# A hybrid recurrent decoder step: a larger filling rate per chunk step, and the late work taken at every step where the filling has run out

## The chip, the cores and the metric

The kernel runs on one core of one Trainium2 chip. The metric is the device time of one execution in microseconds (us). The engines are named as the profile names them: PE is TensorE, DVE is VectorE, ACT is ScalarE, POOL is GpSimd, SP issues DMAs.

## What is computed

Two layers work on 512 prompt tokens with 16 learned tokens ahead of them, and on 8 sample tokens that carry states. Each layer is a half feed-forward, a mixer, and a half feed-forward:

```python
for l in range(DEPTH):                       # DEPTH = 2
    x = x + half_ffn(x, ...)                 # 0.5 * (silu(h @ Wg) * (h @ Wu)) @ Wd
    h = rmsnorm(x, prm['norm_mix'][l])
    m = even_mixer(h, ...) if l % 2 == 0 else odd_mixer(h, ...)
    x = x + m
    x = x + half_ffn(x, ...)

def even_mixer(h, ...):
    proj = h @ even_w_in
    # four gated heads:   S_t = diag(f_t) S_{t-1} + k_t v_t^T,  o_t = S_t^T q_t   (128 x 128)
    oa = rmsnorm(gla_seq(q, k, v, logf, ...) * sigmoid(ga), hgrn_norm)
    # eight RWKV-7 heads: S_t = S_{t-1} diag(w_t) + (S_{t-1}(-kk_t)) (kk_t*a_t)^T + v_t k_t^T,
    #                     y_t = S_t r_t                                            (64 x 64)
    ob = (group_norm(y) + bonus) * g
    return concat([oa, ob]) @ even_w_out
```

All of the change lies in the even mixer of layer 0.

## The kernel before

The 536 tokens lie along the free axis; a matrix product in full precision is three matmuls per 128 x 128 block (high by high, low by high, high by low), over two token parts, 0 to 272 and 272 to 536. On tiles called `d` these triples are the dense products; on tiles `w` lies the RWKV recurrence; on tiles `m` the rest.

**The RWKV recurrence** (`waves`) goes through 9 chunks of tokens (one of 16, eight of 64) for two groups of heads, 18 chunk runs. A chunk run opens with `stage_g` (18 matmuls), then inverts a triangular matrix in ten alternating steps (`lev_t` on PE with ACT copies, `lev_x` on PE with a DVE copy), and ends with five output steps (`st_p`, `st_t`, `st_sa`, `st_s`, `st_y`) that carry the state. Three inverses run side by side, and a table fixes the order: 280 steps, numbered 0 to 279 here. The last chunk run opens in step 240, so from step 241 on ever fewer runs are in flight.

**What is put between the steps.** PE's order is the order in which the code of the loop is written out; the other engines are ordered by a scheduler. After each step the loop earns a credit of `FILL` columns, at most `FILL_MAX`, and spends it on the gated heads (`hgrn_thread`): for heads 0 to 3 a chain of advances (`hcore`, 2500 credit each, 1000 for head 3, that is PE scores, DVE masks and products, POOL scalings), and beside them the dense projections of the next head in pieces of 816 or 792 columns (three matmuls). Heads 0 to 2 have a head's projections beside their advances; head 3 has 12 advances and no projection left. When this thread has ended, what is left of the credit goes to the output projection over the first token part (`mix_out`, 8 weight blocks of 24 matmuls, 192 in all), as soon as two things are done: the norm over the gated heads (`hgrn_norm`, "first" in the code) and the RWKV output work of tokens 0 to 272 ("half").

**Those two are in `post`**, a second thread, which is advanced in every third step and charges `POST` (2000) or a quarter of it. It takes the token spans 0 to 272, 272 to 400 and 400 to 536 as the recurrence passes them; for each span `rpost` does two pairs of head groups in four advances each, and each pair holds two reciprocals on DVE. `hgrn_norm` comes in seven advances: squares of the four heads, a matmul with ones, square root, a reciprocal over all tokens, and four scalings.

After the last step what is left of `post` runs, with the rest of `mix_out` put between its advances, and then the output projection over the second token part (192 matmuls in 8 blocks, with weights loaded anew), and the second feed-forward.

```python
def gla_core(...):                                   # one level of an advance, L651 to L662
    scores(li + 1)                                   # PE, then DVE masks
    nc.vector.tensor_mul(qv[:, :, 1], ...)           # L659
    nc.gpsimd.tensor_mul(kv[:, :, 0], ...)           # L660
    nc.vector.tensor_mul(nxt, ...)                   # L662
```

Of the kernel before, what the change touches and what calls it, by code (L numbers as in the profile page):

```python
# [51 lines left out]
NVEC = _r  # L52


FILL, FILL_MAX = 1100, 5000
CORE, CORE_LAST = 2500, 1000
BESIDE = 2000
AHEAD = 12864
# [3 lines left out]
SAMPLE_EVERY, POST_EVERY = 3, 3  # L62
# [46 lines left out]
def trunk(ctx, tc, A, O):  # L109
# [4 lines left out]
    def til(pool, shape, tag, dt=F32, bufs=None):  # L114
        cnt[0] += 1
        kw = {} if bufs is None else {"bufs": bufs}
        return pool.tile(shape, dt, tag=tag, name=f"{tag}_{cnt[0]}", **kw)
# [8 lines left out]
    def psum(**sizes):  # L126
        if sizes == {tag: n for tag, (_, n) in rings.items()}:
            return
        banks.close()
        rings.clear()  # L130
        for tag, n in sizes.items():
            pool = banks.enter_context(tc.tile_pool(name=f"ps{tag}", bufs=n, space=bass.MemoryType.PSUM))
            rings[tag] = (pool, n)
# [457 lines left out]
    def mix_out(w, norm, l, xd, part, mid=None, units=None):  # L591
        for m in range(NK):
            u = unit(w, 0, 128 * m, NK, 2) if units is None else units(m)
            xv = X['x'][:, m]
            if part != PARTS[1]:
                nc.sync.dma_start(xv, xd[m])  # L596
            yield from dense_steps(u, NK, lambda k: hh[:, k], lambda k: hl[:, k],
                                   lambda ps, sl: nc.vector.tensor_add(xv[:, sl], ps, xv[:, sl]), [part], 1)
            if mid is not None and part != PARTS[1] and m == 1:
                mid()  # L600
        norm_split(norm, l, slice(*part))
# [168 lines left out]
    def even_mixer(rstd, xd, left):  # L770
        w_in = A["even_w_in"][0]
        c0 = 2048
        right = ExitStack()
        mx = right.enter_context(tc.tile_pool(name="mx", bufs=1, side="right"))
        g2 = til(mx, [P, 512], "g2")
        lg = til(mx, [P, T], "lg")
        shl = til(mx, [P, 14, 9], "shl")
        R = [dict(sl=til(mx, [P, 5, T], f"sl{p}"), wc=til(mx, [P, 9], f"wc{p}"),
                  ws=til(mx, [P, NB], f"ws{p}"))
             for p in range(4)]  # L780
        for Q in R:
            Q["r"] = Q["sl"][:, 4]
        oa = [til(mx, [P, T], f"oa{h}") for h in range(4)]
        nc.scalar.dma_start(g2, A["rwkv_g2"][0])
        he = ExitStack()
        hp = he.enter_context(tc.tile_pool(name="hp", bufs=1))
        H = {}
        th = hgrn_thread(hp, rstd, w_in, oa, H)
        psum(d=4, m=4)
        with tc.tile_pool(name="etmp", bufs=1, side="right") as tmp:  # L790
            rwkv_in(tmp, rstd, w_in, c0, g2, lg, shl, R, th)
        psum(d=2, m=2, w=4)
        pb = right.enter_context(tc.tile_pool(name="pb", bufs=1, side="right"))
        ts = chain(*(rsample(R[p], p, lambda i: til(npool, [P, T], ("acc", "sq")[i])) for p in range(4)))
        now = [0]


        def hgrn():
            yield from th
            he.close()  # L800
            xp = left.enter_context(tc.tile_pool(name="xp1", bufs=1))
            X['x'] = til(xp, [P, NK, T], "xT")
            now.append("norm")

        def hgrn_end():
            if "norm" in now and "done" not in now:
                now.append("done")
                for _ in hgrn_norm(oa):
                    yield POST // 4
                now.append("first")  # L810

        def post():
            for span in zip(SPANS, SPANS[1:]):
                while 3 not in H or now[0] < 10 and CHUNKS[max(now[0] - 1, 0)][0] < span[1]:
                    yield from hgrn_end()
                    yield 0
                for _ in ts:
                    yield 0
                for p in (0, 2):
                    yield from hgrn_end()  # L820
                    gens = [rpost(i, R[i], g2, lg, *span) for i in (p, p + 1)]
                    while gens:
                        gens = [g for g in gens if next(g, 0) is None]
                        yield POST
                if span[1] >= PARTS[0][1]:
                    now.append("half")

        with tc.manual_schedule(engines={mybir.EngineType.PE}):
            th_, po = hgrn(), post()
            mo = mix_out(A["even_w_out"][0], "norm_ffn2", 0, xd, PARTS[0])  # L830
            credit = FILL_MAX
            for n, w in enumerate(waves(pb, R)):
                now[0] = w
                if n % SAMPLE_EVERY == 0:
                    next(ts, None)
                if n % POST_EVERY == 0:
                    credit -= next(po, 0)
                credit = min(credit + FILL, FILL_MAX)
                while credit > 0:
                    cost = next(th_, None)  # L840
                    if cost is None and "first" in now and "half" in now:
                        cost = next(mo, None)
                    if cost is None:
                        break
                    credit -= cost
            now[0] = 10
            for _ in th_:
                pass
            for _ in po:
                if "first" in now and "half" in now:  # L850
                    credit = MIX
                    while credit > 0:
                        credit -= next(mo, credit)
            for _ in mo:
                pass
        psum(d=4, m=4)
        for _ in mix_out(A["even_w_out"][0], "norm_ffn2", 0, xd, PARTS[1]):
            pass
        right.close()

    def hgrn_norm(oa):
        yield
        acc = squares(oa)
        yield
        yield
        ro = til(npool, [P, T], "rstd", bufs=2)
        sum_to_rstd(acc, 1.0 / 512, ones, ro)
        for k in range(4):
            nc.vector.tensor_mul(oa[k], oa[k], ro)
            gcol = vec("hgrn_norm", k)  # L870
            nc.scalar.activation(hh[:, k], oa[k], AF.Copy, scale=gcol)
            nc.vector.scalar_tensor_tensor(hl[:, k], oa[k], gcol, hh[:, k].bitcast(F32), ALU.mult, ALU.subtract)
            yield
# [467 lines left out]
    def rpost(p, Q, g2, lg, a, b):  # L1341
        n = b - a
        r, k, v, y = (z[:, a:b] for z in (Q["r"], Q["sl"][:, 1], Q["sl"][:, 2], Q["sl"][:, 3]))

        pair_t = til(npool, [P, 2, 272], ("acc", "sq")[p % 2])[:, :, :n]

        def over(lhsT, rhs, fn):
            wide(lhsT, rhs, lambda ps, sl: fn(ps), [(0, n)], "w")

        yc, sq = pair_t[:, 0], pair_t[:, 1]  # L1350
        over(bones, y, lambda ps: nc.vector.scalar_tensor_tensor(yc, ps, -1.0 / 64, y, ALU.mult, ALU.add))
        yield
        nc.scalar.activation(sq, yc, AF.Square)
        over(bones, sq, lambda ps: nc.scalar.activation(y, ps, AF.Sqrt, bias=epst[:, 1:2], scale=1.0 / 64))
        yield
        nc.vector.reciprocal(y, y)
        nc.vector.scalar_tensor_tensor(r, r, vec("rwkv_rk", p), k, ALU.mult, ALU.mult)
        over(bones, r, lambda ps: nc.vector.tensor_mul(sq, ps, v))
        nc.vector.tensor_mul(yc, yc, y)
        yield  # L1360
        nc.vector.tensor_scalar(yc, yc, vec("rwkv_ln_w", p), vec("rwkv_ln_b", p), ALU.mult, ALU.add)
        nc.vector.tensor_add(yc, yc, sq)
        over(g2[:, 128 * p:128 * p + 128], lg[:, a:b], lambda ps: nc.vector.tensor_mul(yc, ps, yc))
        nc.scalar.copy(hh[:, 4 + p, a:b], yc)
        nc.vector.tensor_sub(hl[:, 4 + p, a:b], yc, hh[:, 4 + p, a:b].bitcast(F32))
# [261 lines left out]
    rstd = norm_in("norm_mix", 0)  # L1627
    left.close()
    even_mixer(rstd, xd, left)
    psum(d=4, m=4)  # L1630
    ffn(0, "ffn2", norm_rstd())
# [98 lines left out]
```

## Time and profile before

| | |
|---|---|
| time, median of 3 runs | 2314.42 us (2308.76 to 2318.76) |
| time of the profiled execution | 2311.46 us |
| its span, first to last instruction | 2309.6 us |
| PE busy | 97% |
| DVE busy | 70% |
| ACT busy | 48% |
| the even mixer, step 0 to the end of its output projection | 520 to 921 us |

Busy is the time in which at least one instruction of the engine was under way. Matmuls overlap each other, so a busy PE can still take more work: a dense matmul of 272 columns is shown with some 0.29 us, and in a row of them one starts every 0.125 us. Every matmul of the program has its record in this trace, so the steps can be counted off line by line: step 207 starts at 780.1 us, step 232 at 822.0, step 255 at 841.5, and the last one ends at 870.4.

### The profile page before, as it was taken

How to read it: one execution, taken by the hardware profiler on the slowest of the kernel's cores; microseconds unless marked ns; L12 is line 12 of the kernel's file. 1: busy time of each engine (PE TensorE's matmuls, PEld its weight loads, DVE VectorE, ACT ScalarE, POOL GpSimd, SP SyncE). 2: the span in 40 equal slices, each digit the busy share in tenths (PEclk: the TensorE clock that was granted, in tenths of full speed). 3: DMA queues.
4: the chain of work that ended last, by engine and by line, in shares of the span. 5: the costliest groups of instructions: out<-in, count | busy, mean ns of one | idle time of the engine just before them, and what ended most of it. 6: DMA issues, size and time to landing. Idle time of an engine off the chain costs nothing. (4 is left out here: it accounts for less than half of the span.)

```text
span 2309.6 us, 52355 instructions
## 1 busy us (share of the span) xinstructions
PE 2242.7 (97%) x22000; PEld 2158.7 (93%) x22000; DVE 1623.5 (70%) x2899; ACT 1098.4 (48%) x2128; POOL 141.9 (6%) x192
## 2 busy tenths in 40 slices
PE   8999999998999989999999999999999989999998
PEld 8999999997788778999999999999999889999998
DVE  7858576686556778966757885857666777948576
ACT  6525254375454556444535452525444464525355
POOL 0000000312212100000000000000021210000000
PEclk9999999998999999999999999999999999999999
DMA  6323334223222115242423332333444453333324
GB/s 171 108 76 101 92 92 132 81 65 95 80 63 81 50 50 166 66 119 83 115 78 101 92 104 79 101 93 89 124 122 125 120 152 92 92 92 101 110 85 136
DMA packets 409412, 229.55 MB, mean 99 GB/s; under 512 B 19252, under 2 KB 400501, under 8 KB 409176
## 3 DMA queue, kind: packets, MB, share of 16 engines
q1 hardware_dynamic: 408456, 224.78, 33.8%
q8 instruction: 173, 2.83, 0.5%
q10 hardware_dynamic: 720, 1.42, 0.2%
q14 instruction: 63, 0.52, 0.1%
HBM read 211.19 MB, written 14.97 MB: 98 GB/s over the span
## 5 line engine op out<-in xcount | busy, mean ns | idle before, releaser
L242 PE MATMUL d<-hh,whi 128*128 128x264 f32 (+2 forms) x1136 | 344.6, 304 | 3.5 <-ACT whi L230 1.5
L244 PE MATMUL d<-hh,wlo 128*128 128x264 f32 (+2 forms) x1136 | 326.0, 288 | 2.1 <-DVE wlo L231 2.1
L243 PE MATMUL d<-hl,whi 128*128 128x264 f32 (+2 forms) x1136 | 326.1, 287 | 0.1
L336 PE MATMUL d<-hh,whi 128*128 128x268 f32 (+1 forms) x832 | 237.7, 286 | 1.7 <-ACT hh L189 1.2
L337 PE MATMUL d<-hl,whi 128*128 128x268 f32 (+1 forms) x832 | 238.1, 287 | 0.9 <-DVE hl L190 0.9
L338 PE MATMUL d<-hh,wlo 128*128 128x268 f32 (+1 forms) x832 | 237.9, 286 | 0.0
L242 PEld LDWEIGHTS d<-hh,whi 128*128 128x128 f32 x1136 | 215.6, 190 | 11.5 <-ACT whi L230 2.4
L244 PEld LDWEIGHTS d<-hh,wlo 128*128 128x128 f32 x1136 | 214.8, 189 | 4.5 <-DVE wlo L231 3.8
L243 PEld LDWEIGHTS d<-hl,whi 128*128 128x128 f32 x1136 | 215.9, 190 | 0.9 <-issue 0.3
L336 PE MATMUL d<-hid,whi 128*128 128x264 f32 (+2 forms) x704 | 201.5, 287 | 0.0
L336 PE MATMUL d<-hid,whix 128*128 128x264 f32 (+2 forms) x704 | 201.1, 286 | 0.0
L337 PE MATMUL d<-hid,whix 128*128 128x264 f32 (+2 forms) x704 | 200.8, 285 | 0.0
L337 PE MATMUL d<-hid,whi 128*128 128x264 f32 (+2 forms) x704 | 200.6, 286 | 0.0
L338 PE MATMUL d<-hid,wlox 128*128 128x264 f32 (+2 forms) x704 | 200.6, 285 | 0.0
L338 PE MATMUL d<-hid,wlo 128*128 128x264 f32 (+2 forms) x704 | 200.5, 285 | 0.0
L536 DVE SCALAR_TENSOR_TENSOR xT<-d,xT 128x272 f32<-128x272 f32 (+2 forms) x192 | 82.9, 433 | 166.9 <-PE d L338 166.9
L336 PE MATMUL d<-sumh,whix 128*128 128x268 f32 (+1 forms) x576 | 170.9, 297 | 0.0
L338 PE MATMUL d<-sumh,wlo 128*128 128x268 f32 (+1 forms) x576 | 164.7, 286 | 0.0
L337 PE MATMUL d<-suml,whix 128*128 128x268 f32 (+1 forms) x576 | 164.3, 285 | 0.0
L336 PE MATMUL d<-sumh,whi 128*128 128x268 f32 (+1 forms) x576 | 164.2, 285 | 0.0
L338 PE MATMUL d<-sumh,wlox 128*128 128x268 f32 (+1 forms) x576 | 164.0, 285 | 0.0
L337 PE MATMUL d<-suml,whi 128*128 128x268 f32 (+1 forms) x576 | 164.0, 285 | 0.0
(386 smaller groups left out, 6438.5 us busy)
## 6 DMA issues: line engine op xcount, KB each, us to landing
raw<-in_ffn_gate_dram SPq DMA_DIRECT2D x44, 512.0 KB
raw<-in_ffn_up_dram SPq DMA_DIRECT2D x44, 512.0 KB
rawx<-in_ffn_gate_dram SPq DMA_DIRECT2D x44, 512.0 KB
rawx<-in_ffn_up_dram SPq DMA_DIRECT2D x44, 512.0 KB
raw<-in_ffn_down_dram SPq DMA_DIRECT2D x32, 512.0 KB
rawx<-in_ffn_down_dram SPq DMA_DIRECT2D x32, 512.0 KB
raw<-in_even_w_in_dram SPq DMA_DIRECT2D x30, 512.0 KB
raw<-in_odd_w_in_dram SPq DMA_DIRECT2D x25, 512.0 KB
```

The costliest lines, as they stand in the source:

```text
L242: nc.tensor.matmul(o, hi[:, k], h, start=(k == 0), stop=False)
L243: nc.tensor.matmul(o, hi[:, k], l, start=False, stop=False)
L244: nc.tensor.matmul(o, lo[:, k], h, start=False, stop=(k == nk - 1))
L336: nc.tensor.matmul(o, hi[:, k], rh(k), start=start and k == 0, stop=False, **kw)
L337: nc.tensor.matmul(o, hi[:, k], rl(k), start=False, stop=False, **kw)
L338: nc.tensor.matmul(o, lo[:, k], rh(k), start=False, stop=stop and k == nk - 1, **kw)
L536: nc.vector.scalar_tensor_tensor(xv[:, sl], ps, -0.5, xv[:, sl], ALU.mult, ALU.add)
```

## The change

Two edits. A step earns 1400 instead of 1100, and `post` is also advanced in a step that finds the credit at its limit of 5000, that is in one where nothing was left to fill it.

```diff
-FILL, FILL_MAX = 1100, 5000
+FILL, FILL_MAX = 1400, 5000
...
-                if n % POST_EVERY == 0:
+
+                if n % POST_EVERY == 0 or credit >= FILL_MAX:
                     credit -= next(po, 0)
                 credit = min(credit + FILL, FILL_MAX)
                 while credit > 0:
```

No instruction is added or removed: PE has the same 18,871 matmuls, in another order. Followed through the loop, the places move like this (steps):

| | before | after |
|---|---|---|
| advances of gated heads 0 to 2, with projections | 0 to 206 | 0 to 161 |
| advances of head 3 | 206 to 231 | 162 to 170 |
| norm over the gated heads | 234 to 252 | 178 to 184 |
| output work of span 0 to 272 | 207 to 228 | 185 to 196 |
| first half of the output projection | 57 of 192 matmuls in 255 to 278, 135 after the last step | all 192 in 197 to 231 |
| output work of span 272 to 400 | 255 to 276 | 234 to 247 |
| steps with nothing between them | 232 to 254, but for the norm | 248 to 278 |
| output work of span 400 to 536 | step 279 and after it | the same |

Three places in the order of the built programs. Names are tile names: `acc`, `sq` and `sl` are tiles of a head pair, `rstd` the norm's factor, `oa` a gated head, `xx`, `gm`, `tm`, `t1c`, `pp`, `pd`, `S` belong to the recurrence, `hh`, `hl` and `whi`, `wlo` are the high and low parts of activations and weights.

**DVE, the norm's reciprocals.** Before, in steps 243 to 250:

```order
L168 RECIPROCAL rstd_11028<-rstd_11028 128x272
L168 RECIPROCAL rstd_11028<-rstd_11028 128x264
L1143 COPY_PREDICATED xx_10292<-cu_67,w_11056 128x2x128
L869 TENSOR_TENSOR oa_619_4521<-oa_619_4521,rstd_11028 128x536
L869 TENSOR_TENSOR oa_620_4522<-oa_620_4522,rstd_11028 128x536
L1283 TENSOR_TENSOR S_1647_11074<-w_11069,S_1545_10491 128x256
L872 SCALAR_TENSOR_TENSOR hl_71<-oa_619_4521,vcol_69,hh_70 128x536
L872 SCALAR_TENSOR_TENSOR hl_71<-oa_620_4522,vcol_69,hh_70 128x536
L1143 COPY_PREDICATED xx_10644<-cu_67,w_11078 128x2x128
```

After the change the same two reciprocals are followed by a subtraction (L1352, `acc`), the products with `oa` 619 to 621 and the low parts of 619 and 620, and then, still in steps 185 to 188:

```order
L873 SCALAR_TENSOR_TENSOR hl_71<-oa_621_4523,vcol_69,hh_70 128x536
L870 TENSOR_TENSOR oa_622_4524<-oa_622_4524,rstd_10239 128x536
L1352 SCALAR_TENSOR_TENSOR sq_10299<-w_10300,sl_610_4512 128x272
L1357 RECIPROCAL sl_607_4509<-sl_607_4509 128x272
L873 SCALAR_TENSOR_TENSOR hl_71<-oa_622_4524,vcol_69,hh_70 128x536
L1360 TENSOR_TENSOR acc_10295<-acc_10295,sl_607_4509 128x272
L1357 RECIPROCAL sl_610_4512<-sl_610_4512 128x272
L1231 COPY xx_9309<-w_10339 64x2x64
```

Before, the recurrence's copies (L1143, L1283) stand between the norm's products; now the whole norm and the first pair's two reciprocals (L1357) stand between the last recurrence copy ahead of them and the next, L1231.

**PE, the same place.** Before, the matmul with ones of the norm (L157 on `acc`) in step 243:

```order
L1214 MATMUL w_11014<-cf_66,xx_10644 128x128 x2
L157 MATMUL m_11029<-acc_10926,cf_66 128x272
L157 MATMUL m_11033<-acc_10926,cf_66 128x264
L1268 MATMUL w_11040<-pp_10998,xx_9941 128x128 x2
L1194 MATMUL w_11045<-xx_10956,gm_10957 32x32 x8
L1194 MATMUL w_11056<-t1c_11001,xx_10292 32x32 x8
L1278 MATMUL w_11069<-tm_9944 128x128
```

and now in step 180, with the first advances of span 0 to 272 (L157 on `sl` and `acc`) a few steps on:

```order
L157 MATMUL m_10240<-acc_10209,cf_66 128x272
L157 MATMUL m_10244<-acc_10209,cf_66 128x264
L1195 MATMUL w_10251<-t1c_10178,xx_9662 32x32 x8
L1195 MATMUL w_10264<-t1c_10199,xx_10113 32x32 x8
L1295 MATMUL w_10277<-gm_8978,sa_10196 64x64 x4
L1207 MATMUL w_10287<-xx_9309,gm_9310 64x64 x2
L1215 MATMUL w_10287<-cf_66,xx_9309 128x128 x2
L157 MATMUL w_10296<-sl_607_4509,cf_66 128x272
L157 MATMUL w_10300<-sl_610_4512,cf_66 128x272
L1195 MATMUL w_10303<-xx_9662,gm_9663 32x32 x8
L1215 MATMUL w_10303<-cf_66,xx_9662 128x128 x2
L157 MATMUL w_10318<-acc_10295,cf_66 128x272
```

What stood some 27 steps apart, with the span's advances first, now follows within seven steps, norm first.

**PE, behind the last step.** Before, from the last advance of step 279:

```order
L157 MATMUL w_11522<-sl_607_4509,cf_66 128x136
L157 MATMUL w_11526<-sl_610_4512,cf_66 128x136
L1335 MATMUL w_11529<-cf_66,S_1709_11414 128x128
L1335 MATMUL w_11535<-cf_66,S_1709_11414 128x128
L1335 MATMUL w_11541<-cf_66,S_1729_11507 128x128
L1335 MATMUL w_11547<-cf_66,S_1729_11507 128x128
L157 MATMUL w_11554<-acc_11521,cf_66 128x136
L157 MATMUL w_11558<-sq_11525,cf_66 128x136
L242 MATMUL d_11471<-hh_70,whi_11463 128x272
L243 MATMUL d_11471<-hl_71,whi_11463 128x272
L244 MATMUL d_11471<-hh_70,wlo_11464 128x272
```

and now:

```order
L157 MATMUL w_11729<-sl_607_4509,cf_66 128x136
L157 MATMUL w_11733<-sl_610_4512,cf_66 128x136
L1336 MATMUL w_11736<-cf_66,S_1737_11670 128x128
L1336 MATMUL w_11742<-cf_66,S_1737_11670 128x128
L1336 MATMUL w_11748<-cf_66,S_1749_11717 128x128
L1336 MATMUL w_11754<-cf_66,S_1749_11717 128x128
L157 MATMUL w_11761<-acc_11728,cf_66 128x136
L157 MATMUL w_11765<-sq_11732,cf_66 128x136
L157 MATMUL w_11770<-sl_607_4509,cf_66 128x136
L157 MATMUL w_11776<-sl_610_4512,cf_66 128x136
L157 MATMUL w_11782<-lg_4507,g_604_4506 128x136
L157 MATMUL w_11789<-lg_4507,g_604_4506 128x136
```

The dense triples (`d`) that stood behind the second `L157` pair have gone to steps 197 to 231. Further on the scheduler puts eight matmuls of the second token part between the last advances; 24 others of them it has put into steps 234 to 246.

## Rows read from the trace of the kernel before

**Rows 1.** The page: span, and busy time of each engine over it.
```profile
span 2309.6 us, 52355 instructions
...
PE 2242.7 (97%) x22000; PEld 2158.7 (93%) x22000; DVE 1623.5 (70%) x2899; ACT 1098.4 (48%) x2128; POOL 141.9 (6%) x192
```

**Rows 2.** Busy time by stretch: us, PE, PEld, DVE, ACT, POOL, granted clock, DMA share, GB/s.
```profile
520.00:780.00 260.00, 243.54 (x4261) 206.82 (x4259) 148.03 (x440) 126.92 (x368) 58.34 (x61) 0.95 0.27 75
780.00:822.00 42.00, 35.19 (x650) 28.75 (x650) 36.94 (x99) 22.73 (x61) 8.04 (x11) 0.92 0.16 44
822.00:842.00 20.00, 15.93 (x317) 12.14 (x314) 16.66 (x37) 11.85 (x34) 0.00 (x0) 0.89 0.33 112
842.00:870.00 28.00, 27.02 (x284) 24.09 (x285) 19.82 (x61) 13.09 (x43) 0.00 (x0) 0.96 0.08 24
870.00:894.00 24.00, 22.41 (x174) 21.45 (x175) 20.84 (x55) 13.85 (x39) 0.00 (x0) 1.00 0.51 146
893.00:921.00 28.00, 25.07 (x195) 24.05 (x195) 20.91 (x37) 17.16 (x31) 0.00 (x0) 1.00 0.74 201
```

**Rows 3.** The same for instructions on tiles w: us, PE, PEld, DVE, ACT, clock.
```profile
520.00:780.00 260.00, 147.44 (x2690) 112.23 (x2690) 58.36 (x201) 59.85 (x201) 0.95 0.27 75
...
822.00:842.00 20.00, 15.19 (x313) 11.49 (x310) 5.52 (x20) 6.31 (x23) 0.89 0.33 112
```

**Rows 4.** The same for tiles m, then for tiles d, over the steps 0 to 206.
```profile
520.00:780.00 260.00, 36.85 (x1040) 28.31 (x1040) 17.75 (x72) 9.33 (x24) 0.95 0.27 75
...
520.00:780.00 260.00, 102.86 (x531) 74.84 (x529) 9.96 (x23) 0.00 (x0) 0.95 0.27 75
```

**Rows 5.** Tiles d in the late stretches, PE first, then PEld, DVE, ACT.
```profile
842.00:870.00 28.00, 10.71 (x57) 8.54 (x57) 0.88 (x2) 0.00 (x0) 0.96 0.08 24
870.00:893.00 23.00, 18.66 (x135) 17.29 (x135) 2.14 (x5) 0.00 (x0) 1.00 0.49 141
```

**Rows 6.** PE in order of time: start, us, instruction, idle before and its releaser.
```profile
794.56 0.23 PE L640 MATMUL m<-hq,hk 128*16 128x16 f32 x2 [3.49 <-DVE oa L914]
...
826.38 0.25 PE L1174 MATMUL w<-sl,bd 128*32 128x32 f32 x8
...
828.95 0.38 PE L1261 MATMUL w<-cf,pd 128*128 128x128 f32 x2
...
835.48 0.45 PE L1294 MATMUL w<-gm,sa 128*64 128x64 f32 x8 [1.67 <-DVE xx L1143]
```

**Rows 7.** DVE in order of time, steps 207 to 254: the same columns.
```profile
781.15 0.44 DVE L1351 SCALAR_TENSOR_TENSOR acc<-w,sl 128x272 f32<-128x272 f32 x1
...
789.55 1.84 DVE L1356 RECIPROCAL sl<-sl 128x272 f32<-128x272 f32 x1
...
831.62 3.51 DVE L168 RECIPROCAL rstd<-rstd 128x272 f32<-128x272 f32 x2 [1.51 <-ACT rstd L167]
835.05 0.38 DVE L1143 COPY_PREDICATED xx<-cu,w 128x256 f32<-128x256 uint8 x1
```

**Rows 8.** POOL in order of time: two key scalings of the fourth gated head.
```profile
800.88 0.66 POOL L660 TENSOR_TENSOR hk<-hk,dlev 128x264 f32<-128x264 f32 x1 [5.00 <-PE m L640]
802.60 0.63 POOL L660 TENSOR_TENSOR hk<-hk,dlev 128x256 f32<-128x256 f32 x1 [1.07 <-PE m L629]
```

**Rows 9.** Waits in 518 to 890 us: who for whom, total us, times, longest.
```profile
DVE sl L1120 <- POOL sq L1118: 7.8, 4, 2.6
```

**Rows 10.** DVE in order of time, after the last step: the last token span.
```profile
870.37 0.30 DVE L1351 SCALAR_TENSOR_TENSOR acc<-w,sl 128x136 f32<-128x136 f32 x1
...
872.47 1.97 DVE L1356 RECIPROCAL sl<-sl 128x136 f32<-128x136 f32 x2 [1.57 <-ACT sl L1354]
...
881.33 0.29 DVE L1351 SCALAR_TENSOR_TENSOR acc<-w,sl 128x136 f32<-128x136 f32 x1
...
891.05 0.29 DVE L1365 TENSOR_TENSOR hl<-sq,hh 128x136 fp32r<-128x136 f32 x1
```

**Rows 11.** PE in order of time: the output projection over the second half.
```profile
893.67 0.36 PE L242 MATMUL d<-hh,whi 128*128 128x264 f32 x1 [1.01 <-DVE xT L598]
```

## The prediction

> **What bounds the kernel now.** First the page: PE is busy for 97% of the span [rows 1], so it can only be order, and not work, that the change wins or loses. All of the change lies in the even mixer, 520 to 921 us, so the second view is busy time by stretch [rows 2]. Four things are to be seen in it. Steps 0 to 206 are full: 243.5 of 260 us, 1.26 us per step. The steps of head 3 (780 to 822) are DVE's: it is busy for 36.9 of 42 us, and PE for 35.2. The steps with nothing between them (822 to 842) are short of work: PE 15.9 of 20 us. The two stretches of dense work at the end run at full clock (1.00), while the others show 0.95, 0.92, 0.89 and 0.96. With levels of 1.2 and 2.4 GHz, a mean of 0.95 is a tenth of the time at the lower one, so that 26 + 6.7 + 4.4 + 2.2, some 39 us, go at half speed, and about half of it, 20 us, is lost there.
>
> The same windows by tile [rows 3, 4] say what a step is. In steps 0 to 206 the recurrence (`w`) shows 147.4 us of PE, the gated heads (`m`) 36.9, dense products (`d`) 102.9. These overlap: their sum is 287.2 and PE's time 243.5, a factor of 0.85. The timelines [rows 6, 7, 8] say who makes PE wait: DVE at both places shown.
>
> **The change part by part.** Nothing is added, so I price the new order stretch by stretch; the old one is 400.6 us (260 + 42 + 20 + 28 + 23.3 + 27.3, the last cut at 893.7 where the second half begins [rows 11]).
>
> (a) Heads 0 to 2 now take 162 steps, not 207. Their own work stays; 45 steps of recurrence drop out from between. What is such a step worth? If it hid behind other PE work: 147.4 x 0.85 / 207 = 0.60 us. By an uncovered one: 20 / 23 = 0.87 [rows 2], of which PE shows 15.2 / 23 = 0.66 on `w` [rows 3]. The filling is thick here, so I lie in the middle: 0.73, the mean of both ends. 260 - 45 x 0.73 = 227 us (221 to 233).
>
> (b) Head 3's 12 advances in some 10 steps, with nothing else between. An advance is a chain PE, DVE, POOL, and two key scalings on POOL start 1.72 us apart [rows 8]: 12 x 1.72 = 20.6. From below: a third of the `m` time, 12.3, and nine steps at 0.71, cut by 0.85, is 16 us of PE. From above: two waits of 3.49 us as at 794.56 [rows 6] on top, 28. I take 20.6, since the POOL rows are of head 3's own advances.
>
> (c) Norm and output work of span 0 to 272, steps 172 to 196. On DVE the norm is 3.51 us of reciprocals [rows 7] and eight operations over 536 columns; one over 272 takes 0.44 [rows 7], so 8 x 0.88 = 7.0. The span has four groups, each a reciprocal of 1.84 and eight operations of 0.44: 4 x 5.36 = 21.4. The recurrence's own DVE work is 5.52 / 23 = 0.24 per step [rows 3], 6.0 for 25. Together 37.9 us of DVE, while PE has 25 x 0.66 = 16.5 and a few matmuls. As the order shows, all of the norm and the first pair's two reciprocals, 3.5 + 7.0 + 3.7 = 14.2 us, stand ahead of the recurrence's copy L1231: the recurrence and all of PE behind it wait there, where before a copy stood between the norm's products and waited for 3.5 us at most. The sample tokens' chain, whose rest falls here too, has made DVE wait for POOL for 2.6 us at most [rows 9]. 37.9 + 2.6 = 40.5; I take 40. Lower bound 30 (14.2, then 20 steps at 0.73 and a little), if the rest of the DVE work runs on beside the dense steps behind it; upper 46, if DVE stays as full as in 780 to 822 (0.88) and waits for POOL besides.
>
> (d) Steps 197 to 231 with all 192 matmuls of the first half. A dense matmul costs 18.66 / 135 = 0.138 [rows 5], 26.5 us, and 35 covered steps at 0.60 are 21: 47.5 us (45 to 51: the step at 0.54, without the tenth that went at half speed, or at the 0.71 that `w` shows uncut, 147.4 / 207). The eight weight blocks (512 KB each, 4 MB in 47 us, 89 GB/s) and the `xT` loads come earlier on SP; 201 GB/s were moved in 893 to 921 [rows 2], so they are hidden. Without that cover PE would wait about 1 us per block, as at 893.67 [rows 11], 8 us.
>
> (e) Steps 232 to 247 with span 272 to 400 and 24 dense matmuls. Before, this span took the 28 us of steps 255 to 278 with 57 matmuls [rows 5]; less 33 x 0.138 and eight steps at 0.60 it is 18.6. I take 19 (17 to 23: DVE alone, 19.8 less 8 x 0.24, is 17.9).
>
> (f) Steps 248 to 278 (and the last) now have nothing between them: 32 steps. None opens a chunk run (an opening takes 2.57 us, from 826.38 to 828.95 [rows 6]) and there is no norm's stall (1.67). (20 - 2 x 2.57 - 1.67) / 21 = 0.63 us: 20 us. From below the covered 0.60, 19; from above 0.87, 28, since with ever fewer runs in flight each waits for its own copies.
>
> (g) The last span after the last step stands alone. Its two pairs took 870.4 to 893.7, 23.3 us, beside 18.7 us of dense matmuls [rows 5, 10]. DVE's own share is four groups of 0.98 + 8 x 0.30 = 3.4, 13.5 us; one wait for ACT as shown, 1.57 [rows 10], makes 15 (13.5 without it, 18 with three). What was covered by PE's work is now a bare chain on DVE.
>
> (h) The second half without the 32 matmuls put ahead: 160 x 25.07 / 195 [rows 2] = 20.6, and a wait of 1.0 [rows 11]: 21.5, where 27.3 stood.
>
> Sum: 227 + 20.6 + 40 + 47.5 + 19 + 20 + 15 + 21.5 = 410.6, that is 10.0 us more. Against the profiled execution's own 2311.46 us (2.9 under the median of 2314.42, which I take as no difference) that is 2321 us (rounded down), 0.3% over the median. A measurement of this kernel can tell about 0.5%, some 11.6 us. In short: 33 us are won in (a), 8 in (g) and 6 in (h); stretches (b) to (f) take 147 us where 780 to 870 took 90, which gives back 57, most of it in (c) and (f), where PE waits for DVE or for the recurrence's own chain. Cover is moved, not made.
>
> **The rivals.** *Faster, thicker filling (R1).* Per step there are now 1400 columns, not 1100. In 0 to 206 PE is idle for 16.5 us and the clock costs 0.05 x 260 = 13. If the denser stretch loses neither, (a) falls by 161/207 of 29.5, that is 23, to 204, and the time is 2298. For it speaks that each step's wait has more columns behind it; against it, that the 3.49 us waits on DVE come from the gated chain, whose advances now come closer, in every 1.8th step and no longer in every 2.3rd. It decides if steps 0 to 161 take less than 212 us.
>
> *Slower, the clock in the bare stretches (R2).* (b), (c), (f) and (g) leave PE with half of its time idle or in short matmuls. The row 822 to 842, the one like them before, shows 0.89, the lowest [rows 2]. In 780 to 822 the lower level stood for 0.08 x 2 x 42 = 6.7 us; if it does so in each of the four, half of it is lost, 4 x 3.4 = 14: 2335. It decides if the granted clock in (b), (c), (f), (g) falls below 0.85.
>
> The Trainium skill (TensorE: Matmul & The Clock Gate, section "HAM oscillation — how this bites in real kernels") says that waits between bursts of matmuls throw the array back to half clock, burst after burst, and that half of the throttled time is lost. That speaks against this change, as (c) makes PE wait for DVE where it had been fed. The trace agrees so far as the stretch with waits has 0.89 and the dense ones 1.00.
>
> *No net change (R3).* DVE's 37.9 us in (c) and POOL's chain in (b) are different engines; if the norm's and the span's DVE work runs on beside (d), (c) is 30 and the sum is as before: 2311. For it: PE's order does not bind DVE. Against it: the copy L1231 stands behind 14.2 us of it. That the change would not move the work at all is excluded by the order of the built programs.
>
> **How the numbers follow.** Forecast, a small loss or none: 0.42, with its own range 2312 to 2330. R1 0.18, R2 0.23, R3 0.17. The predicted time is that of the first, 2321. Bounds added up (221 + 16 + 30 + 45 + 17 + 19 + 13.5 + 20.6 against 233 + 28 + 46 + 51 + 23 + 28 + 18 + 27) are far too wide to hold together; the range goes from R1 to a little over R2 and leaves out only what lies past them: 2298 to 2339. Faster by over 0.5% (under 2303): R1, 0.19 with the tail of R3. Within: R3 and three quarters of the forecast, 0.47. Slower (over 2326): R2 and the rest, 0.34.
>
> **What would show it.** Right: steps 0 to 161 in 221 to 233 us; the norm's reciprocals, eight products and two span reciprocals in a row on DVE with PE idle for several us behind them, released by DVE L1231; a bare stretch of about 20 us before the last step; 15 us from it to the second half. Wrong: a first stretch under 212 us (R1), a stretch (c) near 30, with no idle time of PE over 1 us (R3), or a clock under 0.85 in the bare stretches (R2). The step I trust least is the 0.73 of (a): each 0.1 is 4.5 us.

## The result, and the profile after

The changed kernel takes 2350.68 us (median of 4 runs, 2344.97 to 2353.34) where the kernel before takes 2315.59 (4 runs): a ratio of 1.0152, 95% interval 1.0122 to 1.0183. It is slower by 35 us. The forecast was 2321, the range 2298 to 2339. The profiled execution after took 2353.34 us, 41.9 more than the one before; stretches below are from these two.

The page after, in the form of [rows 1]: PE is busy for 18 us more, and yet for a smaller share of a span that is 42 us longer.

```profile
span 2351.6 us, 52368 instructions
...
PE 2260.5 (96%) x22000; PEld 2170.3 (92%) x22000; DVE 1630.9 (69%) x2899; ACT 1099.9 (47%) x2128; POOL 142.9 (6%) x192
```

Busy time by stretch after, with the columns of [rows 2]. The cuts are the starts of steps 0, 162, 172, 185, 197, 232, 248, the end of the last step, and the end of the output projection.

```profile
519.77:751.45 231.68, 214.38 (x3651) 184.07 (x3650) 133.70 (x391) 106.44 (x300) 53.22 (x56) 0.95 0.29 79
751.45:790.41 38.96, 22.85 (x445) 19.09 (x444) 23.19 (x53) 12.57 (x32) 14.68 (x17) 0.65 0.28 75
790.41:798.76 8.35, 8.28 (x182) 6.62 (x181) 4.71 (x16) 6.68 (x19) 0.00 (x0) 1.00 0.81 263
798.76:826.60 27.84, 20.06 (x194) 13.73 (x191) 26.22 (x49) 13.83 (x39) 0.00 (x0) 0.82 0.00 1
826.60:874.32 47.72, 47.72 (x639) 42.00 (x639) 28.43 (x73) 26.48 (x69) 0.00 (x0) 1.00 0.24 68
874.32:893.23 18.91, 18.22 (x263) 15.30 (x262) 15.67 (x49) 8.95 (x30) 0.00 (x0) 1.00 0.20 58
893.23:918.01 24.78, 20.82 (x301) 16.42 (x301) 9.71 (x35) 10.85 (x36) 0.00 (x0) 0.94 0.01 2
918.01:957.84 39.83, 31.46 (x202) 28.98 (x201) 30.20 (x69) 22.29 (x51) 0.00 (x0) 0.87 0.50 136
```

Two numbers of each row say what a stretch loses: its length less PE's busy time is idle, and the part by which the granted clock falls short of 1, times the length, is what the clock took. The mixer lasts 438.1 us here (519.8 to 957.8) and 400.4 before (520.2 to 920.6). Idle time is 54 us here and 33 by the rows of before, the clock's part 37 and 20. What is left is 347 and 348 us. This count takes time twice in which PE is idle at the lower clock: by the clock's record in the traces 18.5 us of the lower level fall on idle time here, 14.3 of them in (b), and 2.3 before, and half of each is counted in both parts. Counted once, the clock's part is 28 and 18 us, and what is left is 355 and 351. So of the 38 us, 22 are idle time, 10 to 17 the clock, and up to 5 are in neither. By the forecast's letters, with the simple count:

| | forecast | after | lost there: idle + clock |
|---|---|---|---|
| (a) steps 0 to 161 | 227 | 231.7 | 17.3 + 11.6 |
| (b) head 3, steps 162 to 171 | 20.6 | 39.0 | 16.1 + 13.6 |
| (c) norm and span, 172 to 196 | 40 | 36.2 | 7.9 + 5.0 |
| (d) 197 to 231 | 47.5 | 47.7 | 0 |
| (e) 232 to 247 | 19 | 18.9 | 0.7 |
| (f) 248 to 279 | 20 | 24.8 | 4.0 + 1.5 |
| (g) last span | 15 | 14.3 | (g) and (h): 8.4 + 5.2 |
| (h) second half | 21.5 | 25.6 | |

Before, steps 0 to 206 lost 16.5 + 13, head 3's stretch 6.8 + 3.4, and everything behind the last step about 4 and nothing [rows 2]. The 4 us by which the spans differ beyond the mixer were not followed up; 1.6 of them arise in the next weight blocks, and the rest from 1734 us on, in the second layer, which the change leaves as it is.

Head 3's stretch: first the busy time of the part in which the granted clock stays at its lower level (0.50), then PE in order of time. The recurrence's matmuls (`w`) are few, and an advance begins with `L739`, `L629` or `L620`.

```profile
758.06:785.37 27.31, 13.03 (x285) 10.94 (x285) 15.58 (x32) 6.09 (x16) 11.74 (x15) 0.50 0.35 93
```

```profile
759.70 0.65 PE L629 MATMUL m<-hq,hk 128*32 128x32 f32 x32 [2.29 <-POOL hk L660]
...
766.13 0.39 PE L739 MATMUL m<-hq,st 128*32 128x1 f32 x16 [5.75 <-DVE st L755]
...
772.41 0.39 PE L739 MATMUL m<-hq,st 128*32 128x1 f32 x16 [2.34 <-DVE st L755]
...
776.42 0.39 PE L739 MATMUL m<-hq,st 128*32 128x1 f32 x16 [2.93 <-DVE st L755]
```

`L739` is the output of the head's *sample* tokens, of which the forecast's (b) said nothing. Its three waits are 11.0 of the 16.1 us idle. Who delays the first and longest is seen on POOL and then on DVE, in order of time:

```profile
762.19 1.04 POOL L1112 TENSOR_TENSOR sq<-sq,sl 128x512 f32<-128x512 f32 x1 [0.87 <-DMA sq<-dr]
763.31 1.26 POOL L1113 TENSOR_TENSOR acc<-acc,sq 128x512 f32<-128x512 f32 x1
764.53 1.18 POOL L753 TENSOR_TENSOR vb<-vb,hk 128x256 f32<-128x256 f32 x2
```
```profile
765.17 1.15 DVE L755 TENSOR_TENSOR st<-st,vb 128x256 f32<-128x256 f32 x2 [3.57 <-POOL vb L753]
```

The RWKV sample tokens' chain (L1112, L1113) waits for its own DMA and stands ahead of the gated head's `L753` on POOL; DVE's `L755` waits for that, and PE for `L755`. Ahead of the second wait POOL's `L753` stands for its own DMA (`vb`, 1.02 us idle), so that not all three come from the RWKV chain. Before, that chain's last operation on POOL lay at 746.9 us and head 3's first scaling at 783.4: they never met. POOL before, with the last of head 3's scalings:

```profile
746.90 1.28 POOL L1118 TENSOR_TENSOR sq<-acc,sq 128x512 f32<-128x512 f32 x1 [5.22 <-DMA sq<-dr]
783.39 0.87 POOL L660 TENSOR_TENSOR hk<-hk,hf 128x264 f32<-128x264 f32 x1 [35.21 <-PE m L640]
...
811.10 0.62 POOL L660 TENSOR_TENSOR hk<-hk,dlev 128x256 f32<-128x256 f32 x1 [4.32 <-PE m L620]
```

DVE at the norm, steps 185 to 188, in the order that the built program had shown:

```profile
799.32 3.51 DVE L168 RECIPROCAL rstd<-rstd 128x272 f32<-128x272 f32 x2
802.74 0.38 DVE L1352 SCALAR_TENSOR_TENSOR acc<-w,sl 128x272 f32<-128x272 f32 x1
...
807.60 0.43 DVE L1352 SCALAR_TENSOR_TENSOR sq<-w,sl 128x272 f32<-128x272 f32 x1
807.96 1.84 DVE L1357 RECIPROCAL sl<-sl 128x272 f32<-128x272 f32 x1
...
812.44 0.22 DVE L1231 COPY xx<-w 64x128 f32<-64x128 f32 x1
```

and PE beside it. It stands for 7.0 us, behind the span's own matmuls `L157`, whose inputs begin with the two late `L1352`:

```profile
803.64 0.73 PE L157 MATMUL w<-acc,cf 128*128 128x272 f32 x2 [2.52 <-ACT acc L1354]
...
808.83 1.27 PE L157 MATMUL w<-sq,cf 128*128 128x272 f32 x2 [4.47 <-ACT sq L1354]
```

Behind the last step PE waits for the last span, and then for weights:

```profile
932.28 0.81 PE L242 MATMUL d<-hh,whi 128*128 128x264 f32 x2 [2.31 <-ACT hh L1365]
...
943.26 0.39 PE L242 MATMUL d<-hh,whi 128*128 128x264 f32 x1 [1.21 <-ACT whi L230]
...
957.84 0.39 PE L336 MATMUL d<-hh,whi 128*128 128x268 f32 x1 [2.38 <-ACT whi L294]
```

### The profile page after: what moved, and what is told of

The parts are those of the page before. It is cut to its first block, busy times and chain, and to the rows that moved or that the text cites. A ratio compares the mean times of both kernels' runs of the same rounds, so it can differ in the third digit from the quotient of the medians.

```text
span 2351.6 us, 52368 instructions
## 1 busy us (share of the span) xinstructions
PE 2260.5 (96%) x22000; PEld 2170.3 (92%) x22000; DVE 1630.9 (69%) x2899; ACT 1099.9 (47%) x2128; POOL 142.9 (6%) x192
```

## The experiments

Ratios are to the kernel before on the same chip, with their 95% intervals; the changed kernel's is 1.0152. Edits are to the changed kernel where nothing else is said. All rows shown are of busy time by stretch, with the columns of [rows 2].

**One edit at a time.**

```diff
-                if n % POST_EVERY == 0 or credit >= FILL_MAX:
+                if n % POST_EVERY == 0:
```

> FILL is 1400, but the second thread is advanced in every third step alone, as before. Chain theory (an advance of head 3 is a chain over PE, DVE and POOL of some 3 us, and nine steps no longer cover twelve of them): the fourth head still stands in steps 162 to 170, so that stretch takes 35 to 40 us again and the time is 2338 to 2353; the norm, now in steps 183 to 203, gives up to 7 us back. Queue theory (the sample tokens' chain sits on POOL's queue in those very steps): the same. Jam theory (the cost of the change is the norm and the span's reciprocals packed together on DVE): most of the 35 us is gone, 2318 to 2328.

Measured: 1.0121 (1.0096 to 1.0147), 2339.16 us, in the range of chain and queue. Head 3's stretch again takes 39.4 us. Norm and span lose 12.4 us over steps 172 to 227, against 12.9 in the 25 steps of the changed kernel: packing them changed nothing there. The jam theory fell as the main cause. The interval overlaps that of the change.

```diff
-FILL, FILL_MAX = 1400, 5000
+FILL, FILL_MAX = 1100, 5000
```

> FILL is 1100 as before, and the second thread is also advanced where the credit is at its limit. Chain and queue theory: head 3 keeps its steps 206 to 231 and the span's work beside it, so nothing is lost there; the norm takes steps 234 to 242 and the first half of the output projection begins at step 243 and not 255, 108 of its matmuls before the last step: 2303 to 2318. Jam theory: the norm alone is packed, its eight products and two reciprocals (10 us of DVE) stand ahead of the recurrence's copies: 2322 to 2340.

Measured: 1.0045 (1.0029 to 1.0062), 2317.52 us, at the upper end of the first forecast, and slower beyond its interval. The rows of steps 232 to 242 (the norm), 243 to 279, and behind the last step:

```profile
817.63:830.34 12.71, 10.30 (x158) 7.68 (x149) 10.12 (x21) 5.94 (x16) 0.00 (x0) 0.87 0.51 175
830.34:878.37 48.03, 44.28 (x503) 37.84 (x503) 30.29 (x85) 21.80 (x64) 0.00 (x0) 0.93 0.14 42
878.37:927.32 48.95, 42.31 (x311) 39.93 (x310) 36.23 (x79) 26.73 (x60) 0.00 (x0) 0.97 0.55 151
```

The norm's 11 steps lose 2.4 + 1.7 us, no more than the 23 steps 232 to 254 before (4.1 + 2.2, [rows 2]). But the steps behind it lose 3.8 + 3.4, so that 232 to 279 lose 11.2 us together, where they lost 8.4. What it brought forward, 51 matmuls of the first half, is missed behind the last step: 6.6 + 1.5 us are lost there, against about 4.

**What makes head 3's stretch long.**

```diff
-SAMPLE_EVERY, POST_EVERY = 3, 3
+SAMPLE_EVERY, POST_EVERY = 2, 3
```

> The changed kernel with the sample tokens' chain advanced in every second step, so that it has ended before step 162. Queue theory: POOL is free for head 3, steps 162 to 171 fall from 39 to some 21 us, and the time is 2328 to 2335. Chain theory: they still take 30 us or more and the time is 2338 to 2350. Jam theory: no difference, 2345 to 2353.

Measured: 1.0174 (1.0149 to 1.0200), 2349.8 us. The stretch:

```profile
746.87:781.91 35.04, 25.90 (x445) 21.90 (x445) 18.40 (x51) 10.92 (x29) 7.82 (x11) 0.61 0.19 54
```

It takes 35.0 us, 4 less, so the chain theory's range held and the queue theory's 21 fell. The time shows no gain, as the norm's steps 182 to 193 take 30.8 us here, 3 more.

```diff
-gens = [gla_step(...), gla_core(...)]
+gens = ([gla_step(...)] if h < 3 else []) + [gla_core(...)]
```

> The changed kernel without the sample tokens' step of the fourth gated head (their states are not advanced and their outputs lack it); its twelve advances over the prompt stay. Step theory (the three waits for DVE L755, 11.0 us, hold the stretch up): steps 162 to 171 take 20 to 26 us, not 39, and the time is 2328 to 2338. Level theory (the levels' own chain over PE, DVE and POOL is what lasts): 33 to 38 us, 2343 to 2352.

Measured: 1.0110 (1.0085 to 1.0135), 2334.15 us, and the stretch:

```profile
744.84:775.55 30.71, 21.06 (x380) 17.60 (x380) 19.19 (x47) 12.46 (x32) 11.84 (x12) 0.72 0.21 56
```

That is 8.3 less, neither theory's number; the time lies in the step theory's range. This kernel leaves out the sample outputs and states of head 3. Both edits together:

> The changed kernel without the fourth head's sample step (its states are not advanced, its outputs lack it) and with the sample tokens' chain ended before step 162, so that steps 162 to 171 hold the twelve levels and the recurrence alone. If the levels by themselves go as fast as the shortest spacing of 1.72 us on POOL: 19 to 23 us, and 2318 to 2328. If they are a chain of 2.2 us or more each: 26 to 31 us, 2328 to 2338.

Measured: 1.0108 (1.0080 to 1.0136), 2338.35 us. The stretch:

```profile
749.06:776.82 27.76, 21.03 (x380) 17.54 (x379) 15.24 (x41) 10.57 (x28) 5.02 (x7) 0.75 0.08 24
```

27.8 us: the twelve advances over the prompt, with ten steps of recurrence beside them, are 2.3 us each, and not 1.72. On top come 7 to 8 us of the head's sample step and 3 to 4 of the sample chain on POOL: 27.8 + 7.2 + 4.0 = 39.0. These shares are rough: the same instructions of this stretch took 37.7, 39.4 and 42.0 us in the profiles of three other runs (the norm on POOL, `FILL` alone, the first half begun late). The whole is not in doubt, for none came near 28. The time gains nothing over the last run, as the norm's steps 182 to 193 take 31.6 us here, 4 more than in the changed kernel.

Is the low clock a cost of its own? Two products without a reader behind each of head 3's advances:

```diff
+                if h == 3:
+                    for _ in range(2):
+                        jk = bank()
+                        nc.tensor.matmul(jk[:, :272], ones, maskg[:, :272], start=True, stop=True)
                 yield CORE if h < 3 else CORE_LAST
```

> The changed kernel with two products of 272 columns more behind each advance of head 3, whose result nobody reads (24 in all, some 13 us of PE at full clock), so that PE has work while it would wait. Clock theory (the lower clock of 0.65 there is a cost of its own, 13.6 us): the clock stays near 1.00 and the stretch falls to 28 to 34 us, the time to 2338 to 2346. Wait theory (the low clock only stretches work that lies in waits anyway): 38 to 44 us, 2349 to 2358.

Measured: 1.0176 (1.0150 to 1.0202), 2349.84 us. The stretch:

```profile
749.18:793.61 44.43, 38.38 (x494) 26.88 (x493) 24.16 (x54) 12.74 (x32) 15.04 (x17) 0.81 0.25 70
```

PE is idle for 6 us and not 16, the clock is 0.81 and not 0.65, and the stretch is 5 us longer. The wait theory holds, as far as this run goes: the clock did not stay near 1.00, so what a full clock would give was not seen, and the added products, some 13 us by the expectation's estimate, stand on PE between the chain's own matmuls.

```diff
-CORE, CORE_LAST = 2500, 1000
+CORE, CORE_LAST = 2500, 4000
```

> The changed kernel with 4000 credits for an advance of head 3 and not 1000: its twelve advances lie in steps 162 to 207 with the span's output work beside the later ones. Chain theory: each advance is covered by some four steps, the stretch of 46 steps takes 50 to 60 us where 172 to 207 and the head took 39 and more with it, and the time is 2305 to 2325. Queue theory: POOL still has the sample tokens' chain beside the first advances, 2335 to 2350. Jam theory: norm still packed (steps 210 to 218), 2335 to 2350.

Measured: 1.0118 (1.0097 to 1.0140), 2337.16 us; above the chain theory's range, and in that of the other two. Steps 162 to 207 take 61 us, within the 50 to 60 expected but for 1, and lose 14.5:

```profile
751.46:766.39 14.93, 10.53 (x269) 8.49 (x269) 10.74 (x27) 7.68 (x22) 8.33 (x9) 0.98 0.40 108
766.39:783.71 17.32, 15.08 (x320) 12.12 (x321) 11.73 (x36) 6.83 (x21) 6.86 (x8) 0.72 0.25 72
783.71:812.57 28.86, 26.16 (x371) 19.59 (x367) 22.52 (x55) 15.91 (x47) 0.00 (x0) 1.00 0.18 56
...
905.31:945.80 40.49, 31.52 (x203) 28.93 (x201) 30.23 (x69) 22.48 (x53) 0.00 (x0) 0.87 0.49 133
```

The head was one cost, then, but not the whole. PE still waits 4.9 us ahead of `L739`, and the steps of the packed norm (208 to 218) lose 2.9 + 2.9. The last row shows another: the bare end loses 9.0 + 5.3 us.

**DVE at the norm.**

```diff
-            nc.vector.tensor_mul(oa[k], oa[k], ro)
+            nc.gpsimd.tensor_mul(oa[k], oa[k], ro)
```

> The changed kernel with the norm's four products with the factor (L870) on POOL, which is idle then, and not on DVE. Jam theory (what stands on DVE ahead of the recurrence's copy sets the end in steps 185 to 196): 2.7 us less on DVE, 27.8 falls to 24 to 26 us, and the time to 2345 to 2349. Rival: POOL is slower at it and the low parts on DVE wait for POOL, so that the same copy comes no earlier: 2350 to 2355.

Measured: 1.0189 (1.0160 to 1.0219), 2352.63 us, and steps 185 to 196 take 30.6 us. The rival was right: POOL needs 1.52 us for a product of 0.71, the low parts wait for it, and the copy `L1231`, 13.7 us behind the start of step 185 in the changed kernel, comes 14.7 behind it here.

```profile
799.93 6.08 POOL L870 TENSOR_TENSOR oa<-oa,rstd 128x536 f32<-128x536 f32 x4 [21.44 <-DVE rstd L168]
```
```profile
803.33 1.51 DVE L873 SCALAR_TENSOR_TENSOR hl<-oa,vcol,hh 128x536 fp32r<-128x536 f32 x1 [0.24 <-ACT hh L872]
...
810.46 0.28 DVE L1231 COPY xx<-w 64x128 f32<-64x128 f32 x1 [1.10 <-PE w L1230]
```

**The bare end.** First half begun late (step 258), 69 of its matmuls behind the last step:

```diff
-                    if cost is None and "first" in now and "half" in now:
+                    if cost is None and "first" in now and "half" in now and n >= 258:
```

> The changed kernel with the first half begun no earlier than step 258, 69 of its 192 matmuls behind the last step. End theory: idle time and clock behind the last step fall from 13.6 to some 6 us, the bare steps take back less: 2338 to 2345. Cover theory: what the end wins the bare steps lose, 2346 to 2356.

Measured: 1.0118 (1.0092 to 1.0143), 2335.56 us, 2.4 under the end theory's range. Rows of steps 197 to 231, now with nothing between them, and of the end:

```profile
822.72:844.46 21.74, 20.73 (x447) 17.02 (x447) 13.86 (x46) 14.56 (x46) 0.00 (x0) 1.00 0.01 3
...
897.58:943.13 45.55, 40.16 (x295) 37.86 (x294) 35.56 (x80) 25.88 (x59) 0.00 (x0) 0.96 0.57 158
```

The end theory holds in the rows: 5.4 + 1.8 us are lost there, not 13.6. And 35 bare steps take 21.7 us, 0.62 each, with 1.0 us idle and the clock at 1.00. A bare step in the middle loses nothing.

**All together.** Spread head and unpacked norm; then with the first half held until step 267; then with the sample chain in every second step too:

```diff
-CORE, CORE_LAST = 2500, 1000
+CORE, CORE_LAST = 2500, 4000
...
-                if n % POST_EVERY == 0 or credit >= FILL_MAX:
+                if n % POST_EVERY == 0:
```

> FILL 1400, no packing of the second thread, 4000 credits for an advance of head 3: head 3 in steps 162 to 207 beside span 0 to 272, norm in 210 to 230 in every third step, first half of the output projection in 231 to 276, none of it behind the last step. If the costs of the lone head (some 8 us by one run) and of the packed norm (some 7 by another) add up: 1.006 to 1.010 of the time before. If they are one cost seen twice: 1.010 to 1.013. If 1400 columns by themselves cost nothing: 0.997 to 1.004. What stays above 1 by idle time and clock behind the last step (13 to 14 us in all runs with an empty end, 3.9 before) is the price of the bare end.

Measured: 1.0081 (1.0059 to 1.0103), 2325.7 us. The costs add up; the end still loses 11.0 us.

> As the last one, but the first half of the output projection begins no earlier than step 267, so that 117 of its 192 matmuls stand behind the last step again and steps 231 to 266 have nothing between them. End theory: the loss behind the last step falls from some 14 to 4 us and the bare steps cost 0.27 each, 36 of them 10: no change against the last one within 5 us. Cover theory (a bare step costs as much as its waits and clock, 0.5 us and more): 8 us or more slower than the last one.

Measured: 1.0056 (1.0035 to 1.0077), 2319.56 us, 6 us faster than the last one, a little more than the end theory's 5. The end loses 3.6 us and nothing by the clock.

> FILL 1400 with head 3 spread, the norm in every third step, the first half held until step 267, and the sample tokens' chain in every second step. If that chain beside head 3 (steps 162 to 176) makes up what is still lost: 0.998 to 1.002 of the time before. If not, and the 45 steps taken out of the filling cost later what they saved: 1.004 to 1.008.

Measured: 1.0011 (0.9997 to 1.0026), 2315.2 us. Steps 162 to 207, without and with the quicker sample chain (two kernels, one row each):

```profile
750.92:812.09 61.17, 51.36 (x953) 40.08 (x952) 44.99 (x116) 30.44 (x89) 15.40 (x17) 0.92 0.26 73
```
```profile
750.02:806.46 56.44, 49.95 (x954) 38.46 (x953) 43.90 (x119) 32.90 (x93) 7.55 (x11) 0.94 0.14 41
```

POOL's share falls by 8 us and the stretch by 4.7. The ratio falls by 0.45%, some 10 us, so that half of the gain has no place in these steps. With these four undone, 1400 columns are as good as 1100, and no better.

**Three tries at something faster**, all on the kernel before. Thinner filling (`FILL = 1000`):

> The kernel before with 1000 columns per step and not 1100: heads 0 to 2 last until step 226, head 3 until 262, norm and first half come at and behind the end. If waits belong to the gated heads' advances, and every step only needs some cover (no matter when), the mixer lasts 395 to 405 us as before, 2300 to 2318. If thin filling makes the waits longer: 2320 to 2335. If the loss per uncovered step is what counts, there are fewer of them and it is faster: 2290 to 2300.

Measured: 1.0054 (1.0034 to 1.0074), 2320.98 us, in the range given for longer waits; but by the rows norm and first half come so late that 9.1 us are lost behind the last step and 7.7 in the 17 steps ahead of it.

```diff
-FILL, FILL_MAX = 1100, 5000
-CORE, CORE_LAST = 2500, 1000
+FILL, FILL_MAX = 1200, 5000
+CORE, CORE_LAST = 2500, 2400
...
-                while 3 not in H or now[0] < 10 and ...
+                while now[0] < 10 and ...
```

> The kernel before with the span's output work allowed from step 173 on, before head 3 is ready, 1200 columns per step and 2400 credits for an advance of head 3: the span's DVE work (21 us) lies beside the full steps 173 to 207, where DVE is busy for 0.53, head 3 in 199 to 226, the norm from 228. If DVE's 0.88 in head 3's stretch was what cost 10 us there: 0.995 to 0.999 of the time before. If head 3's own chain lasts as long without it: 0.999 to 1.004. If the full steps pay for the DVE work in waits of the recurrence: 1.003 to 1.010.

Measured: 1.0067 (1.0049 to 1.0085), in the third range, but not for its reason: steps 162 to 198, which take up the span's work, are idle for 0.9 us at a clock of 1.00. Head 3's stretch loses 8.2 us where it lost 10, and with 90 of the first half's matmuls ahead of it (57 before) the end loses 9.0. And with all of the first half behind the last step (`n >= 280` in the condition above):

> The kernel before with no matmul of the output projection's first half ahead of the last step: steps 255 to 278 have only the span's work, and all 192 stand behind the last step. If dense work is worth more there than beside steps: 0.996 to 0.999. If the late steps, with fewer chunk runs in flight, need it as much: 0.999 to 1.003. If the end has cover enough with 135 and the 57 are added to it uncovered, while the late steps stay as long: 1.003 to 1.006.

Measured: 1.0020 (1.0006 to 1.0034), in the second range. The end takes 57.6 us, 7.4 more, and the late steps 24.6 where they took 28.9: the last steps, unlike those in the middle, hide some of the dense work, 3 of 7.4 us.

## Why the prediction was wrong

The mechanism was named: "Cover is moved, not made." The direction of the forecast, a small loss, was right, and its size wrong, by 30 us. Of the 27.5 by which the mixer (438.1) exceeds the forecast's 410.6, (b) is 18.4; (a), (f) and (h) are 4 to 5 each, and (c) gives 4 back. The 4 us outside the mixer come on top.

**The step that failed is (b).** It priced an advance of head 3 at 1.72 us, the spacing of two POOL scalings in [rows 8], "since the POOL rows are of head 3's own advances", and gave 28 as the upper end. It took 39.0. The two rows of POOL were the closest pair; head 3's seven scalings had lain from 783.4 to 811.1 us before, 4.6 apart, and the row shown has 5.00 us idle ahead of it. The twelve advances over the prompt take 2.3 us each (27.8 in all, already the forecast's upper end of 28), the head's sample step, which the sum did not have, adds 7 to 8 and the RWKV sample chain 3 to 4, each as far as the spread of this stretch allows. The forecast put that chain into (c) instead, at 2.6 us; it follows the step's number, and in step 162 it had not ended, as it had in step 206. In the kernel before, the same chain of waits lay beside 26 steps and the span's work, and cost 10 us.

**(a), (d), (e), (g) held** within 5 us: 231.7, 47.7, 18.9 and 14.3 us. The choice of 0.73 per step in (a) looks a little high: (260 - 231.7) / 45 = 0.63, and a bare step elsewhere costs 0.62. But the stretch lasts 225.5 to 231.7 us in the nine profiles that have these steps, and steps 0 to 206 last 251.5 to 259.9 in the three with the order of before, so that a step lies between 0.44 and 0.77. If it is near 0.62, filling faster wins nothing: a step taken out from between dense work saves what it costs later on. The upper end of 0.87, from [rows 2], had the norm's stall and the clock in it.

**(c) came out at 36.2, not 40**, with DVE busy for 0.94 of steps 185 to 196 and PE standing for 7.0 us there, as forecast; but PE waited for the span's statistics, not for the recurrence behind `L1231`, and the loss is no larger than with the norm spread out. The norm's eight operations took 5.5 us, not 7.0. **(f)** is 24.8, not 20: in 248 to 279 PE waits for the last runs' own copies (4.0 idle), within the bounds given. **(h)** is 25.6, not 21.5: the high parts of weights come late from ACT (the last two waits above), and the clock is at 0.93 from 932 us to its end.

**The rivals.** R1 fell: the stretch took 225.5 us or more in every profile, and not under 212. Its 162 steps lose 28.9 us and the 207 of before 29.5 (22.6 and 18.7 in the runs with the first half held). That this loss goes with the gated heads' advances, whose number is the same, is shown for its idle time alone: 14.8 of the 16.5 us before lie ahead of matmuls on tiles `m`. R3 fell: (b) and (c) took 75 us together, where it had said 51. R2 happened in part: the clock takes 10 us more than before (17 with the idle time at the lower clock), R2 had said 14; below its 0.85 are (b), 0.65, and the later part of (c), 0.82, and it is 0.74 in 918 to 932. How much of (b) is the clock's alone stays open: with more work on PE it rose to 0.81 and the time did not fall.

The Trainium skill (TensorE: Matmul & The Clock Gate, section "HAM oscillation — how this bites in real kernels") was right on the direction: where PE waits between bursts, the array falls to half clock. Here 16.1 us idle go with 0.65, and the full stretch (d) shows 1.00.

**Where the 35 us went**, by undoing one thing after another: head 3 spread and norm unpacked, 0.71% (1.0152 to 1.0081); first half held for the end, 0.25%; sample chain in every second step, 0.45%, of which head 3's steps show half; left, 0.11%, whose interval includes no difference at all. Each difference is uncertain by some 0.3%, so their order is less sure than their sum. What the packing alone costs is not settled: by the rows of the run with packing alone some 3 us in steps 232 to 279, behind the norm and not at it, and 4 us behind the last step, for the dense work that it brings forward.

## What to carry to other kernels

Price a chain that is moved into the open by the whole of its length where it lay (first link to last, all side chains with it), not by its closest pair of links. Ask of each stretch what it loses by idle time and by clock, not how busy it is, and count idle time at the lower clock once: here PE's own time was 355 us and 351 before, steps with three inverses in flight lost next to nothing bare, and only the chains through DVE, POOL and DMA (a lone head, the norm, the last span) needed the dense work that the change spent elsewhere. A helper that is paced by a step's number meets other work as soon as the steps are filled differently.

## What the runs showed of the hardware

The same instructions in steps 0 to 161 took 206.4 us in the profile of the kernel before (clock 0.94) and 198.0 where only the end was edited (0.97): one profile's stretch there is good to some 8 us. The clock can stay low while PE is busy: 0.81 with PE busy for 38.4 of 44.4 us. DVE slows beside POOL: the low part `L873`, 0.68 us with POOL idle, took 1.51 while POOL multiplied (`L870`, 6.08 us for four).
